# A feed-forward in 256x1024 weight tiles with tokens on partitions, and Strassen's seven products for some of the tiles

## The chip, the cores and the metric

The kernel runs on one core of one Trainium2 chip. The time is device time in microseconds (us) of one launch. The core's engines run beside each other, each through its own list of instructions in order: TensorE (PE) multiplies 128x128 blocks (a load of the stationary block, PEld, and a matmul that moves up to 512 columns past it) and adds the result up in PSUM, eight banks of 512 float32 columns; VectorE (DVE) and ScalarE (ACT) do elementwise work; SyncE (SP) issues most transfers. An instruction that needs another engine's result waits for a semaphore, and all that stands behind it on its engine waits too.

## The reference

An encoder of two layers over 256 tokens of width 2048, in float32. Each layer is an attention (a 2-D neighbourhood attention in layer 0, a dilated one in layer 1) and a feed-forward of width 8192, each with a norm ahead of it and a residual, and a last norm stands at the end:

```
def sq_relu_mlp(h, w1, w2):
    return jnp.square(jax.nn.relu(h @ w1)) @ w2
...
        x = x + sq_relu_mlp(rms_norm(x, g), w1, w2)
    return rms_norm(x, final_norm)
```

"Matrix one" below is w1 (2048 x 8192), "matrix two" w2 (8192 x 2048).

## The kernel before

**Steps.** All large products are a list of 400 steps. A step loads one block of 512 x 512 weights (1 MB, stored as four slices of 128 x 512) and multiplies with it in four quarters: 48 steps for q, k, v and 16 for the output of layer 0's attention, 72 and 8 for layer 1's, and 128 for each feed-forward. The loop at line 736 writes the program out in this order; each engine takes its instructions in that order, and nothing reorders them. Beside a step's quarters stand its tasks (a part on TensorE, then a part on the other engines), `evac` (reading of finished sums) and `post`.

**Float32 from rounded parts.** [...] A product is hi x hi + hi x lo + lo x hi. `split` (lines 103 to 105) does the cut: ACT rounds, DVE subtracts. For the weights `prep(i, u)` cuts half a block, 1024 columns at a time; in step i the two halves of step i + 2 are cut, the first after the second quarter, the second at the end. The parts lie in four buffers each (`wh`, `wl`), two steps' worth, so a cast for step i + 2 waits until TensorE has read step i's half. Then `load(i + 5)` issues the transfer of a later block, into one of three buffers.

**Matrix one** (`gemm_cols`, lines 114 to 150): the weights stand still and the tokens move. For each 128 x 128 block of weights there is a matmul of 512 columns (hi weights against both parts of the 256 tokens, line 134) and one of 256 (lo weights against hi tokens, line 136): 16 such pairs a step. Four steps sum up 512 of the 8192 hidden columns, which come out with the hidden index on partitions, as matrix two needs them. ACT copies one half of the sum (line 144), DVE adds the other (146), scales by 1/rms and takes the relu (471), ACT squares (474) and both cut the result.

**Matrix two** (`gemm_rows`, lines 160 to 175, `products`, 152): the activations stand still and 512 columns of weights move: three matmuls (lines 155 to 157) for each of two halves of the tokens and four slices, 24 a step. `add_rows` adds the sums to x (line 271).

**Order.** `ffn` (line 464) works in four groups: 16 steps of matrix one make 2048 hidden columns, 16 of matrix two use them up. At the end of a sublayer `pending_norm` transposes x for the next norm (line 194) beside the following steps; `Norm.rows` (229) multiplies to lay 1/rms along the tokens. The last two steps of all go through the first half of the tokens and then the second (`rows_apart`), and `Final.finish` (from 667) finishes a half with the last norm and writes it out.

Of the kernel before, what the change touches and what calls it, by code (L numbers as in the profile page):

```python
# [14 lines left out]
P = 128  # L15
# [13 lines left out]
class Step:  # L29
    """One weight block [4 x 128, 512], the products that it takes part in (in four  # L30
    quarters) and the work that goes with them: tasks have a part on the tensor engine
    after a quarter, evac reads the finished sums, post follows."""

    def __init__(self, src, quarters):
        self.src = src
        self.quarters = quarters
        self.evac = []
        self.tasks = [[] for _ in range(4)]
        self.post = []


@with_exitstack
def tile_encoder(ctx: ExitStack, tc: tile.TileContext, ins, out):
    nc = tc.nc

    const = ctx.enter_context(tc.tile_pool(name="const", bufs=1))
    wpool = ctx.enter_context(tc.tile_pool(name="wpool", bufs=3))
    hlpool = ctx.enter_context(tc.tile_pool(name="hlpool", bufs=4))
    big = ctx.enter_context(tc.tile_pool(name="big", bufs=9))
    mid = ctx.enter_context(tc.tile_pool(name="mid", bufs=9))  # L50
    tmp = ctx.enter_context(tc.tile_pool(name="tmp", bufs=2))
    small = ctx.enter_context(tc.tile_pool(name="small", bufs=4))
    ps_acc = ctx.enter_context(tc.tile_pool(name="ps_acc", bufs=3, space=bass.MemoryType.PSUM))
    ps_misc = ctx.enter_context(tc.tile_pool(name="ps_misc", bufs=2, space=bass.MemoryType.PSUM))
# [11 lines left out]
    rope_c = const.tile([32, T], F32, name="rope_c")  # L66
    rope_s = const.tile([32, T], F32, name="rope_s")
# [4 lines left out]
    steps = []  # L72

    def load(i):
        if i >= len(steps):
            return
        s = steps[i]
        s.w = wpool.tile([P, 4, 512], F32, name="w", tag="w")
        s.hi, s.lo = [None] * 2, [None] * 2
        if i:  # L80
            nc.sync.dma_start(s.w, s.src)

    def load_half(i, u):
        nc.sync.dma_start(steps[i].w[:, 2 * u:2 * u + 2, :], steps[i].src[:, 2 * u:2 * u + 2, :])

    def prep(i, u):
        if i >= len(steps):
            return
        s = steps[i]
        hi = hlpool.tile([P, 2, 512], F32R, name="wh", tag="wh")  # L90
        lo = hlpool.tile([P, 2, 512], F32R, name="wl", tag="wl")
        part = s.w[:, 2 * u:2 * u + 2, :]
        if i:
            split(hi, lo, part)
        else:
            for a in range(2):
                split(hi[:, a], lo[:, a], part[:, a])
        s.hi[u], s.lo[u] = hi, lo
# [15 lines left out]
    def gemm_cols(w, col, xT, nk, done):  # L114
        acc = {}
        made = []
        for k in range(nk):
            def quarter(s, n, k=k):
                if k == 0:
                    if s is steps[0]:  # L120
                        n = (0, 2, 1, 3)[n]
                    if n % 2 == 0:
                        acc[n // 2] = ps_acc.tile([P, 2, 512], F32, name="acc", tag="acc")
# [3 lines left out]
                for j in js:  # L127
                    o = acc[j // 2][:, j % 2, :]
                    cs = slice(j * P, (j + 1) * P)
                    for a in parts:  # L130
# [3 lines left out]
                        nc.tensor.matmul(o, s.hi[a // 2][:, a % 2, cs], xt.rearrange("p h t -> p (h t)"),  # L134
                                         start=first, stop=False)
                        nc.tensor.matmul(o[:, :T], s.lo[a // 2][:, a % 2, cs], xt[:, 0, :],  # L136
                                         start=False, stop=last)
            s = Step(block(w, k, col), quarter)
            steps.append(s)
            made.append(s)  # L140
        for j in range(2):
            def ev(j=j):
                b = tmp.tile([P, 2, T], F32, name="b", tag="b", bufs=2)
                nc.scalar.copy(b, acc[j][:, :, T:])  # L144
                z = tmp.tile([P, 2, T], F32, name="z", tag="z", bufs=2)
# [6 lines left out]
    def products(o, s, xt, a, ts_, start, stop):  # L152
        xh, xl = xt[:, a, 0, ts_], xt[:, a, 1, ts_]
        wh, wl = s.hi[a // 2][:, a % 2, :], s.lo[a // 2][:, a % 2, :]
        nc.tensor.matmul(o, xh, wh, start=start, stop=False)  # L155
        nc.tensor.matmul(o, xh, wl, start=False, stop=False)  # L156
        nc.tensor.matmul(o, xl, wh, start=False, stop=stop)  # L157

# [1 line left out]
    def gemm_rows(w, col, xT, ks, acc, first_k, last_k, apart=False):  # L160
        made = []
        for k in ks:
            def quarter(s, a, k=k):
                if k == first_k and a == 0:
                    tiles = [ps_acc.tile([P, 2, 512], F32, name="acc", tag="acc") for _ in range(1 + apart)]
                    for tb in range(2):
                        acc[tb] = tiles[tb * apart][:, tb, :]
# [3 lines left out]
            s = Step(block(w, k, col), quarter)  # L171
# [5 lines left out]
    class Norm:  # L177
        def __init__(self, n, perm):
            self.n, self.perm = n, perm
            self.xT = [None] * NB  # L180
            self.ss = small.tile([P, 2, NB], F32, name="ss", tag="ss", bufs=2)

        def squares(self, c):
            for tb in range(2):
                junk = tmp.tile([P, 512], F32, name="junk", tag="p", bufs=5)
# [3 lines left out]
        def transposes(self, c, half):  # L189
            self.tp = ps_misc.tile([P, 2, T], F32, name="misc", tag="misc")  # L190
# [5 lines left out]
        def parts(self, c, half):  # L196
            if half == 0:
                self.xT[c] = big.tile([P, 4, 2, T], F32R, name="xT", tag="big")
            xT = self.xT[c]
            for which, a in [(which, 2 * half + a) for which in ("hi", "lo") for a in range(2)]:  # L200
# [9 lines left out]
                elif self.perm:  # L210
                    gx = tmp.tile([P, T], F32, name="gx", tag="p", bufs=5)
# [8 lines left out]
        def rstd(self):  # L220
            r = rsqrt_mean(self.ss)
            self.r = r
            self.rw = tmp.tile([P, 2, P], F32, name="rw", tag="p", bufs=5)
            nc.vector.tensor_copy(self.rw, r.unsqueeze(2).to_broadcast([P, 2, P]))

        def rows(self):
            self.bc_ps = ps_misc.tile([P, 2, T], F32, name="misc", tag="misc")
# [4 lines left out]
        def rows_out(self):  # L232
            self.bc = small.tile([P, T], F32, name="rbc", tag="rbc", bufs=2)
# [6 lines left out]
        def cols(self):  # L240
            self.r_ps = ps_misc.tile([P, 2, T], F32, name="misc", tag="misc")
# [23 lines left out]
    # x += rows; at the end of a sublayer the next norm is begun  # L265
    def add_rows(made, col_block, acc, norm, chunk_done):
        cs = slice(col_block * 512, (col_block + 1) * 512)
        if norm is not None and norm() in fin and col_block == NB - 1:
            return
# [20 lines left out]
    def pending_norm(get):  # L290
        """Hooks behind the steps that finish x's column blocks."""
        def chunk_done(step, c):
            i = steps.index(step)
            for half in range(2):
                at(i + 1, lambda half=half: get().transposes(c, half), lambda half=half: get().parts(c, half),
                   quarter=1 + half)
            if c == NB - 1:
                at(i, None, lambda: get().rstd())
                at(i + 2, lambda: get().rows(), lambda: get().rows_out())
# [11 lines left out]
    def split_v(acc, r):  # L311
        hi = mid.tile([P, 2, 512], F32R, name="v", tag="mid")
        lo = mid.tile([P, 2, 512], F32R, name="v", tag="mid")
# [7 lines left out]
    class NaHeads:  # L321
        """Four heads: their q, k, v, bias and the steps from scores to outputs."""
# [4 lines left out]
        # bias[c + 64 e, h, o, 63 - c'] is for the query (2 t + e, c) and the key (o - 2 + 2 t, c')  # L327
        def load_bias(self, h):
            if h == 0:
                self.bias = big.tile([P, 4, 6, GRID_W], F32, name="bias", tag="big")  # L330
# [10 lines left out]
        def qk(self, which):  # L341
            t = [mid.tile([P, 4, T], F32R, name="qk", tag="mid") for _ in range(2)]
# [15 lines left out]
        def s1_pe(self, h):  # L358
            s = ps_misc.tile([P, 2, T], F32, name="misc", tag="misc")
# [5 lines left out]
        def s1_post(self, h):  # L365
            p = tmp.tile([P, 2, T], F32, name="p", tag="p", bufs=5)
# [7 lines left out]
        def s2_pe(self, h):  # L374
            pt = ps_misc.tile([P, 2, T], F32, name="misc", tag="misc")
# [6 lines left out]
        def s2_post(self, h):  # L382
            t = [tmp.tile([P, 2, T], F32R, name="pT", tag="p", bufs=5) for _ in range(2)]
# [3 lines left out]
        def s3_pe(self, h):  # L387
            o = ps_misc.tile([P, 2, T], F32, name="misc", tag="misc")
# [6 lines left out]
        def s3_post(self, h):  # L395
            if na_oT[self.c] is None:
                na_oT[self.c] = big.tile([P, 4, 2, T], F32R, name="oT", tag="big")
# [3 lines left out]
    def softmax(p):  # L401
        """p [P, 2, n]: each row of n becomes its softmax."""
# [32 lines left out]
    def rows_apart(pair, xT, acc, finish):  # L435
        """The last two blocks of a sum of four: the first half of the tokens through both, then the second."""
        for tb, s in enumerate(pair):
            def quarter(s, n, tb=tb):
                for a in (n % 2 * 2, n % 2 * 2 + 1):
                    products(acc[tb], pair[n // 2], xT[2 + n // 2], a, slice(tb * P, (tb + 1) * P),  # L440
                             False, n == 3 and a == 3)
            s.quarters = quarter
            s.evac.append(lambda tb=tb: finish(tb, acc))

    def out_rows(w, xT, nk, norm, chunk_done, order=None):
        accs = [{} for _ in range(NB)]
        last = norm is not None and norm() in fin
        order = order or [(c, k) for c in range(NB) for k in range(nk)]
# [382 lines left out]
```

## Time and profile before

| | us |
|---|---|
| median of 3 runs (2321.46 to 2324.35) | 2321.56 |
| span of the profiled execution | 2320.3 |
| TensorE waiting for the rests of weights, whole run | 3.4 |
| first feed-forward, from 408 to 1120 us | 712 |
| second feed-forward, from 1603 to 2311 us | 708 |

The runs time the execution as a whole, the span goes from the first to the last instruction. Busy times of TensorE are not additive: matmuls overlap, and one of 512 columns is busy for some 0.39 us while the next starts 0.23 us after it. A line of a view gives the line of the code, the engine, the operation, and the tiles that it writes and reads; after the bar stand busy time, mean duration and the idle time before it with what ended it.

### The profile page before, as it was taken

Reading aid. Unit: us, or ns where it says so; the run is one execution under the profiler, and the core shown is the slowest. Engines: PE = TensorE matmul, PEld = TensorE weight load, DVE = VectorE, ACT = ScalarE, POOL = GpSimd, SP = SyncE. Lnnn points to the kernel's source line nnn. Section 1 sums busy time; section 2 is a strip of 40 time slices with the busy share of each in tenths; the row PEclk is TensorE's granted clock in tenths of the full one; section 3 lists DMA queues with packets and bytes.
Section 4 is the critical chain, followed back from the end, with each engine's and each line's share of the span. In section 5 each row is a group of like instructions: output and inputs, shape, how many; then the busy total and the mean of one; then the engine's idle time right before and its main releaser. Section 6 shows DMA issues by size and latency. Waiting matters only on the chain.

```text
span 2320.3 us, 29178 instructions
## 1 busy us (share of the span) xinstructions
PE 2300.7 (99%) x11956; PEld 1963.1 (85%) x11956; DVE 1406.0 (61%) x1635; ACT 1092.6 (47%) x1390; POOL 0.7 (0%) x6
## 2 busy tenths in 40 slices
PE   8999999999999999999999999999999999999998
PEld 7888888888888888888888888888888888888886
DVE  6666765654555555566777667756654654555654
ACT  6444545543443453455444544445543543543443
POOL 0000000000000000000000000000000000000000
PEclk9999999999999999999999999999999999999999
DMA  7555655555555555555555545454555555555553
GB/s 248 169 175 176 191 182 170 182 197 200 182 187 194 185 196 189 193 181 188 189 179 184 177 164 181 164 181 169 191 192 193 182 200 187 189 187 200 200 192 135
DMA packets 73862, 430.36 MB, mean 185 GB/s; under 512 B 19776, under 2 KB 20352, under 8 KB 22528
## 3 DMA queue, kind: packets, MB, share of 16 engines
q1 hardware_dynamic: 73056, 426.80, 54.3%
q8 instruction: 93, 1.52, 0.3%
q10 hardware_dynamic: 672, 1.70, 0.2%
q14 instruction: 41, 0.34, 0.0%
HBM read 426.38 MB, written 2.10 MB: 185 GB/s over the span
## 4 chain that ended last, share of the span: by engine, by line
PE 98%; DMA 1%; DVE 1%; ACT 0%; issue 0%; SPq 0%; ACTq 0%; DVEq 0%
PE acc L134 33%; PE acc L136 17%; PE acc L156 15%; PE acc L155 15%; PE acc L157 15%; PE misc L194 1%; DMA bias<-in_rpb_dram 0%; PE misc L111 0%; PE misc L110 0%; PE misc L109 0%; DVE wl L105 0%; PE misc L593 0%; PE misc L553 0%; PE misc L380 0%; ACT wh L104 0%
## 5 line engine op out<-in xcount | busy, mean ns | idle before, releaser
L105 DVE TENSOR_TENSOR wl<-w,wh 128x1024 fp32r<-128x1024 f32 (+1 forms) x802 | 972.8, 1221 | 735.8 <-ACT wh L104 733.6
L104 ACT CAST wh<-w 128x1024 fp32r<-128x1024 f32 (+1 forms) x802 | 834.9, 1049 | 936.9 <-PE acc L157 460.2
L134 PE MATMUL acc<-xT,wh 128*128 128x512 f32 x3328 | 1178.5, 399 | 0.9 <-ACT wh L104 0.9
L136 PE MATMUL acc<-xT,wl 128*128 128x256 f32 x3328 | 935.0, 281 | 2.3 <-DVE wl L105 2.3
L134 PEld LDWEIGHTS acc<-xT,wh 128*128 128x128 f32 x3328 | 626.4, 188 | 150.4 <-ACT wh L104 1.9
L136 PEld LDWEIGHTS acc<-xT,wl 128*128 128x128 f32 x3328 | 629.8, 189 | 3.7 <-DVE wl L105 3.2
L155 PE MATMUL acc<-wh,hT 128*128 128x512 f32 x1024 | 399.5, 390 | 0.0
L156 PE MATMUL acc<-wl,hT 128*128 128x512 f32 x1024 | 399.0, 390 | 0.0
L157 PE MATMUL acc<-wh,hT 128*128 128x512 f32 x1024 | 398.9, 390 | 0.0
L157 PEld LDWEIGHTS acc<-wh,hT 128*128 128x128 f32 x1024 | 192.3, 188 | 39.9
L155 PEld LDWEIGHTS acc<-wh,hT 128*128 128x128 f32 x1024 | 192.3, 188 | 39.7
L156 PEld LDWEIGHTS acc<-wl,hT 128*128 128x128 f32 x1024 | 192.3, 188 | 39.4
L155 PE MATMUL acc<-wh,xT 128*128 128x512 f32 x320 | 126.7, 396 | 0.0
L156 PE MATMUL acc<-wl,xT 128*128 128x512 f32 x320 | 125.2, 391 | 1.1 <-DVE wl L105 1.1
L157 PE MATMUL acc<-wh,xT 128*128 128x512 f32 x320 | 124.9, 390 | 0.0
L144 ACT COPY b<-acc 128x512 f32<-128x512 f32 x104 | 60.7, 586 | 64.8 <-PE acc L136 59.1
L146 DVE TENSOR_TENSOR z<-acc,b 128x512 f32<-128x512 f32 x104 | 71.5, 691 | 25.8 <-ACT b L144 25.2
L155 PE MATMUL acc<-wh,oT 128*128 128x512 f32 x192 | 76.6, 399 | 0.0
L157 PE MATMUL acc<-wh,oT 128*128 128x512 f32 x192 | 75.0, 391 | 0.0
L156 PE MATMUL acc<-wl,oT 128*128 128x512 f32 x192 | 74.9, 390 | 0.0
L156 PEld LDWEIGHTS acc<-wl,xT 128*128 128x128 f32 x320 | 60.2, 188 | 13.1 <-DVE wl L105 1.8
L157 PEld LDWEIGHTS acc<-wh,xT 128*128 128x128 f32 x320 | 60.1, 188 | 12.5
(123 smaller groups left out, 1044.9 us busy)
## 6 DMA issues: line engine op xcount, KB each, us to landing
w<-in_ffn_w_dram SPq DMA_DIRECT2D x256, 1024.0 KB, 4.8
w<-in_dil_wqkv_dram SPq DMA_DIRECT2D x72, 1024.0 KB, 4.8
w<-in_na_wqkv_dram SPq DMA_DIRECT2D x47, 1024.0 KB, 4.9
w<-in_na_wo_dram SPq DMA_DIRECT2D x16, 1024.0 KB, 4.9
w<-in_dil_wo_dram SPq DMA_DIRECT2D x8, 1024.0 KB, 4.8
bias<-in_rpb_dram SPq DMA_DIRECT2D x32, 96.0 KB, 8.7
out_dram<-x SPq DMA_DIRECT2D x8, 256.0 KB, 2.5
x<-in_x_dram SPq DMA_DIRECT2D x3, 512.0 KB, 7.8
```

The costliest lines, as they stand in the source:

```text
L104: nc.scalar.copy(dst_hi, src)
L105: nc.vector.tensor_tensor(out=dst_lo, in0=src, in1=dst_hi.bitcast(F32), op=ALU.subtract)
L134: nc.tensor.matmul(o, s.hi[a // 2][:, a % 2, cs], xt.rearrange("p h t -> p (h t)"), start=first, stop=False)
L136: nc.tensor.matmul(o[:, :T], s.lo[a // 2][:, a % 2, cs], xt[:, 0, :], start=False, stop=last)
L144: nc.scalar.copy(b, acc[j][:, :, T:])
L146: nc.vector.tensor_tensor(out=z, in0=acc[j][:, :, :T], in1=b, op=ALU.add)
L155: nc.tensor.matmul(o, xh, wh, start=start, stop=False)
L156: nc.tensor.matmul(o, xh, wl, start=False, stop=False)
L157: nc.tensor.matmul(o, xl, wh, start=False, stop=stop)
L194: nc.tensor.transpose(self.tp[:, a, tb * P:(tb + 1) * P], x[:, tb, kt * P:(kt + 1) * P], ident)
```

## The change

Only the feed-forwards compute differently; around them buffers are laid out anew.

- **Tiles.** A step's 1 MB is now a piece of 256 x 1024 (a pair of 128-row slices k, by two blocks of 512 columns), in two transfers of 512 KB. Eight such steps sum over 2048 rows for 1024 columns and all 256 tokens (`gemm_pair`). Both matrices are multiplied with the tokens on the partitions of the result: activations stand still, weights move.
- **Plain steps** (kind "s") have the 24 matmuls of matrix two before. Their weights are cut as before.
- **Strassen steps** (kind "x") treat the tile as a 2 x 2 block matrix against 2 x 2 blocks of activations (two halves of the tokens, two slices k) and form seven block products for eight: 21 matmuls of 512 columns in quarters of 6, 6, 6 and 3. They use Winograd's sums: four of weights (`prep_x`) and three of activations (`sums_and_parts`). In matrix one the tiles 3 and 5 of each eight are Strassen steps, in matrix two 3, 5 and 6. In matrix two's second block of a group the order of the tiles is 0, 3, 1, 5, 2, 6, 4, 7; layer 0's last group keeps the plain order there, and layer 1's last has 0, 3, 1, 5, 6, 2, 4, 7.
- **`prep`** is spread over a step: for an x tile of step i + 2 the sums after quarter 0 of step i, its own second half and the rounding of the sums after quarter 1, their rest after quarter 2, the slice left over at the end.
- **PSUM.** All eight banks are in use: four for the block sums that plain products add to, four for products that Strassen's scheme combines. After the last x step `begin` combines them into a tile C, in the last step `end` adds the others quarter by quarter. Before, sums came in three pairs of banks and two single ones served the transposes; in the feed-forward these now borrow banks.
- **Hidden values** come out with tokens on partitions: ACT scales by 1/rms, takes the relu and squares, in the first step of the next block; in its second and third step TensorE transposes them in four groups of four, and they are cut, for tiles 3, 5 and 6 with the sums. The multiplication that laid 1/rms along the tokens remains for layer 1's attention and layer 0's first norm alone.
- **Buffers** of attention and feed-forward are now two pools that take each other's place (`Part`).

```
     def prep_x(s, n):
         w = s.w
         if n == 0:
             t = s.sums = part.pool.tile([P, 4, 512], F32, name="sums", tag="sums", bufs=1)
             add(nc.vector, t[:, 0:2, :], w[:, 1:3, :], w[:, 0, :].unsqueeze(1).to_broadcast([P, 2, 512]))
             add(nc.vector, t[:, 2, :], t[:, 1, :], w[:, 1, :])
             add(nc.vector, t[:, 3, :], t[:, 2, :], w[:, 3, :])
         elif n == 1:
             hi, lo = two_parts(s, 1)
             split(hi, lo, w[:, 2:4, :])
             s.hs = part.pool.tile([P, 4, 512], F32R, name="hs", tag="hs", bufs=2)
             nc.scalar.copy(s.hs, s.sums)
         elif n == 2:
             ls = part.pool.tile([P, 4, 512], F32R, name="ls", tag="ls", bufs=2)
             subtract(nc.vector, ls, s.sums, s.hs.bitcast(F32))
...
         else:
             hi, lo = two_parts(s, 0)
             split(hi[:, 1, :], lo[:, 1, :], w[:, 1, :])
...
     X = (("1", "A11", 2), ("2", "A12", 3), ("6", "S2", 6), ("7", "S3", 4), ("5", "S1", 5), ("4", "A22", 7),
          ("3", "S4", 1))
...
             if kind == "x":
                 def quarter(s, m, pair=pair, n=n):
                     for bank, a, b in X[2 * m:2 * m + 2]:
                         product(bank, left(pair, a), (s.hi[b], s.lo[b]), n == first_x[-1] and bank in "1567")
...
     def begin(m):
         if m == 0:
             C = q["C"] = part.pool.tile([P, 4, 512], F32, name="C", tag="C")
             nc.scalar.copy(C[:, 0, :], q["1"])
             q["U"] = scratch([P, 512], "U")
             subtract(nc.vector, q["U"], q["6"], C[:, 0, :])
         elif m == 1:
             subtract(nc.vector, q["C"][:, 2, :], q["U"], q["7"])
...
     s = made[first_x[-1] + 1]
     for m in range(4):
         s.after[0 if s is made[-1] else m].append(lambda m=m: begin(m))
         if not split_end:
             made[-1].after[m].append(lambda m=m: end(m))
...
 def sums_and_parts(raw, t, half, sums):
     c = scratch([P, 3, P], "c")
     a11, a21, a12, a22 = raw[:, 0, :P], raw[:, 0, P:], raw[:, 1, :P], raw[:, 1, P:]
     subtract(nc.vector, c[:, 0, :], a11, a21)
     subtract(nc.vector, a21, a21, a22)
     subtract(nc.vector, c[:, 1, :], a11, a21)
     subtract(nc.vector, c[:, 2, :], a12, c[:, 1, :])
     hi, lo = (t[:, 2 * half:2 * half + 2, h, :] for h in range(2))
     nc.scalar.copy(hi, raw)
     nc.scalar.copy(sums[:, 0], c)
     subtract(nc.vector, lo, raw, hi.bitcast(F32))
     subtract(nc.vector, sums[:, 1], c, sums[:, 0].bitcast(F32))
...
 FF_PAIRS, FF_PAIRS2 = (3, 5), (3, 5, 6)
...
         for n in range(4):
             s.quarters(s, n)
             for pe, post in s.tasks[n]:
                 pe()
+            for f in s.after[n]:
+                f()
...
+            elif i and n < 3:
+                prep(i + 2, n)
             for pe, post in s.tasks[n]:
                 post()
```

More of the change, by code (lines that the diff above doesn't have):

```diff
@@ L482, in tile_encoder, with both @@
+            def both(q, tb):
+                return q["C"][:, 2 * tb:2 * tb + 2, :].rearrange("p a n -> p (a n)")
+            for cp in range(2):
+                end = last and next_norm() in fin and cp == 1
+                order = (0, 3, 1, 5, 6, 2, 4, 7) if end else (0, 3, 1, 5, 2, 6, 4, 7) if cp and not last else range(8)
+                gemm_pair(w2g, cp, hT, sums, ff_order(FF_PAIRS2, order),
+                          lambda made, q, cp=cp: residual(made, q, cp), split_end=end)
     ffn(norms[1], ins["ffn0_w1"], ins["ffn0_w2"], lambda: norms[2], begin_norm(2, True))
+    parts[len(steps)] = "attention"
@@ L736, in tile_encoder @@
     for i, s in enumerate(steps):
+        now["i"] = i
+        if i in parts:
+            part.begin(parts[i])
         if i == 1:
```

420 lines of the change are left out of this document (294 added, 126 removed).

## The prediction

> **What bounds the kernel now.** I read the page first: span, busy times, chain.
>
> ```profile
> span 2320.3 us, 29178 instructions
> ...
> PE 2300.7 (99%) x11956; PEld 1963.1 (85%) x11956; DVE 1406.0 (61%) x1635; ACT 1092.6 (47%) x1390; POOL 0.7 (0%) x6
> ...
> PE 98%; DMA 1%; DVE 1%; ACT 0%; issue 0%; SPq 0%; ACTq 0%; DVEq 0%
> ```
>
> TensorE carries 98% of the chain. The execution took 1.3 us less inside its span than the median of 2321.56, so I subtract from the median. Then the windows (columns: length; busy and count of PE, PEld, DVE, ACT, POOL; clock; DMA): the first feed-forward, and the worst stretch of the attention.
>
> ```profile
> 408.00:1120.00 712.00, 712.00 (x3619) 604.97 (x3618) 405.70 (x421) 331.46 (x387) 0.00 (x0) 1.00 0.55 189
> 73.00:81.00 8.00, 6.49 (x28) 4.58 (x27) 6.65 (x10) 2.98 (x6) 0.00 (x0) 1.00 0.03 13
> ```
>
> In the feed-forward TensorE never stops, VectorE (DVE) has 57% and ScalarE (ACT) 47%. So the time there is a number of matrix products times their spacing, as long as DVE delivers the weights' second parts. Spacings come from the DVE timeline, where sums leave at the end of every fourth step (start, length, line, tiles):
>
> ```profile
> 430.77 1.39 DVE L146 TENSOR_TENSOR z<-acc,b 128x512 f32<-128x512 f32 x2 [0.51 <-ACT b L144]
> 452.95 1.39 DVE L146 TENSOR_TENSOR z<-acc,b 128x512 f32<-128x512 f32 x2 [0.50 <-ACT b L144]
> ...
> 519.19 1.28 DVE L271 TENSOR_TENSOR x<-x,acc 128x512 f32<-128x512 f32 x2 [0.41 <-PE acc L157]
> ...
> 584.47 1.28 DVE L271 TENSOR_TENSOR x<-x,acc 128x512 f32<-128x512 f32 x2 [0.41 <-PE acc L157]
> 606.98 1.40 DVE L146 TENSOR_TENSOR z<-acc,b 128x512 f32<-128x512 f32 x2 [0.55 <-ACT b L144]
> ...
> 674.82 1.41 DVE L146 TENSOR_TENSOR z<-acc,b 128x512 f32<-128x512 f32 x2 [0.55 <-ACT b L144]
> ```
>
> Matrix one takes 22.18 us per four steps in the first group and (674.82 - 606.98)/3 = 22.61 in later ones. Matrix two takes (584.47 - 519.19)/3 = 21.76 for 96 products of 512 columns: 0.2267 us each, 5.44 a step.
>
> **The change: TensorE.** A layer now takes 4 x 22.18 + 12 x 22.61 + 16 x 21.76 = 708.2 us. Afterwards every product has matrix two's form. A plain step has 24, a Strassen step 21 (4.76 us). Matrix one has 16 Strassen steps of 64 a layer: 1488 products; matrix two 24 of 64: 1464. 2952 x 0.2267 = 669.1. The hidden values now have tokens on partitions and must be transposed: 32 groups of four a layer. The chain shows one such group, and the broadcast of 1/rms that norms 1 and 3 no longer need:
>
> ```profile
> 1054.39 0.44 PE misc L194 x4
> ...
> 416.49 0.45 PE misc L229 x4
> ```
>
> 32 x 0.44 = 14.1, so 683.2 a layer: 25.0 saved, 50.0 in two layers, and 2 x 0.45 for the broadcasts: **51 us**. If nothing else changed, 2270.5.
>
> **The change: DVE and ACT.** A plain tile costs each engine two passes of 1024 columns. A Strassen tile needs sums of weights (1024, 512, 512 columns on DVE), their rounding (2048, ACT) and rest (2048, DVE), and 1024 + 512 of its own. Durations by form (us busy, mean ns), then the timeline for what back-to-back instructions take:
>
> ```profile
> L105 DVE TENSOR_TENSOR wl<-w,wh 128x1024 fp32r<-128x1024 f32 x798 | 970.2, 1223 | 735.8 <-ACT wh L104 733.6
> L105 DVE TENSOR_TENSOR hT<-z,hT 128x512 fp32r<-128x512 f32 x64 | 41.4, 689 | 38.7 <-ACT hT L104 38.7
> L368 DVE TENSOR_TENSOR p<-misc,bias 128x256 f32<-128x256 f32 x32 | 12.0, 417 | 0.0
> L338 DVE TENSOR_TENSOR bias<-bias,namask 128x1536 f32<-128x1536 f32 x4 | 7.0, 1758 | 23.4 <-DMA bias<-in_rpb_dram 15.8 <-DMA w<-in_na_wqkv_dram 7.6
> ```
>
> ```profile
> 436.04 1.29 DVE L105 TENSOR_TENSOR hT<-z,hT 128x512 fp32r<-128x512 f32 x2 [1.21 <-ACT hT L104]
> 437.52 2.36 DVE L105 TENSOR_TENSOR wl<-w,wh 128x1024 fp32r<-128x1024 f32 x2 [0.18 <-ACT wh L104]
> ...
> 1140.43 0.29 DVE L496 TENSOR_SCALAR ra<-rbc 128x256 f32<-128x256 f32 x1
> 1140.75 0.42 DVE L497 TENSOR_TENSOR rb<-ra,rope_s 32x256 f32<-32x256 f32 x1
> ```
>
> ```profile
> L104 ACT CAST wh<-w 128x1024 fp32r<-128x1024 f32 x798 | 832.6, 1051 | 936.9 <-PE acc L157 460.2 <-PE acc L134 452.4 <-issue 9.2
> ...
> L474 ACT ACTIVATE z<-z 128x512 f32<-128x512 f32 x64 | 39.5, 633 | 60.6 <-DVE z L471 60.6
> ...
> L104 ACT CAST wh<-w 128x512 fp32r<-128x512 f32 x4 | 2.3, 623 | 0.0
> ...
> L690 ACT ACTIVATE x<-x,fr 128x512 f32<-128x512 f32 x4 | 2.7, 716 | 1.4 <-DVE fr L680 1.4
> ```
>
> Independent instructions overlap: 1024 columns cost 2.36 - 1.22 = 1.14, 512 cost 1.29 - 0.69 = 0.60. One that reads its forerunner's result costs its full length plus 0.03. No row has 2048 columns: 1536 less 1024 is 0.535, so 1.758 + 0.535 = 2.29, 2.21 overlapped. 128 columns: 0.417 - (0.689 - 0.417)/2 = 0.28. ACT's 2048: 1.05 + 2 x 0.43 = 1.91.
>
> [...]
>
> A plain tile: 2.28. A Strassen tile: sums 2.6, own rest 1.14, the 2048 rest 2.21, last 0.60 = 6.55; and the big rest waits for ACT, which starts on the sums at 2.7 and ends at 4.6 while DVE is free at 3.74: 0.89 of waiting, 7.44. Behind that wait on DVE stand the tile's last part and the next tile; TensorE waits for both. TensorE gains 0.68 for it.
>
> The stretch that decides is matrix two. Block A (steps 0 to 7, Strassen at 3, 5, 6) and B (8 to 15, at 9, 11, 13). Preparation runs two steps ahead. Step 0: ACT does eight relu and square passes (pairs of about 1.28), then the last cast of tile 2, so DVE leaves step 0 at 9.3 us, 3.9 after TensorE (5.44). DVE from there: step 1, tile 3, one transposed part (0.60, inside the wait) and one with sums (four of 128, one of 512, one of 384: 2.2) 9.67; step 2, 2.23 + 0.60 + 2.28 = 5.11; steps 3 and 4, tiles 5 and 6, 14.88; step 5, 2.28; step 6, 2.28 + 0.5 waiting for TensorE; step 7, where Strassen's recombination (2.52), the bank sums (2.40), the residual (2.28) and tile 9 (6.55) meet, 13.75; step 8, 2.28; step 9, tile 11 to the end of the big rest, 6.93. Sum 57.7, of which 3.5 are waits.
>
> TensorE would reach tile 11's second quarter after six plain steps, four Strassen steps, four transposes and 1.6: 32.6 + 19.0 + 1.8 + 1.6 = 55.0. So it is delayed 3.9 + 57.7 - 55.0 = **6.6 us a group**; with no wait counted 3.1. Smaller delays within (step 6, the last transposed bank at step 3) lie inside this. Matrix one: 33.5 a block on DVE (4 more with transposed parts) against 186 x 0.2267 = 42.2; no delay.
>
> I take the middle, 4.85: rows with full waits (1.21) are of a DVE that is ahead, the row of one behind (437.52) has 0.18; neither is nearer. 8 x 4.85 = 38.8. The last group of each layer has the next norm's work beside block B (6.9 and 2.4 us of DVE): I add 5 together. Tail:
>
> ```profile
> 2305.91 0.69 DVE L669 TENSOR_TENSOR x<-x,acc 128x512 f32<-128x512 f32 x1 [3.13 <-PE acc L157]
> ...
> 2308.92 0.74 DVE L687 SCALAR_TENSOR_TENSOR x<-x,fr,gf 128x512 f32<-128x512 f32 x1
> 2311.34 0.69 DVE L669 TENSOR_TENSOR x<-x,acc 128x512 f32<-128x512 f32 x1 [1.68 <-PE acc L157]
> ```
>
> The first half's finish holds DVE 3.75 us and began 5.43 before the second; it will begin 2.72 before: 1.0 more. 2321.6 - 51 + 38.8 + 5 + 1 = **2315**.
>
> At nothing I cost: loads (two of 512 KB for one of 1 MB), queued on SP behind the freed tile:
>
> ```profile
> w<-in_ffn_w_dram SPq DMA_DIRECT2D x256, 1024.0 KB, 4.8
> ```
>
> They land in 4.8, and DVE comes to the tile two steps of its own, about 10 us, later; uncovered, each late load costs the difference. ACT's added passes: below 60%, behind DVE in the stretch. The pools that change hands: attention's order is the same; between 0 and 5 us.
>
> **Rivals.** *DVE keeps up.* The gain stays whole: 2321.6 - 51 + 1 = 2272, with delays at the layers' ends some 2276. For it: matrix two averages 40.9 of DVE a block (3 x 7.44 + 5 x 2.28 + 7.2) against 41.5. Against it: block A's 5.7 of transposed parts and the lag of 3.9.
>
> *DVE bounds matrix two, every wait in full* (slower): 8 x 6.6 + 7 = 60, so 2331, to 2342 with DVE 3% slower. It decides from 6.2 us a group, where the 51 are used up. For it: waits for ACT are the commonest wait of DVE now (733.6 us). Against it: only three of the waits have nothing to fill them.
>
> *The clock falls in the gaps.*
>
> ```profile
> 2290.00:2321.00 31.00, 21.31 (x95) 17.31 (x93) 13.49 (x25) 10.61 (x19) 0.00 (x0) 0.90 0.20 76
> ```
>
> With 9.7 us idle the clock is 0.90; in the window from 73 to 81, with 1.5 idle, 1.00. Half speed for as long as the 6.6 idle would add some 50: 2380. [...]
>
> That the products don't get fewer can't be: the order of steps fixes them.
>
> **How the numbers follow.** A measurement of this kernel can tell about 0.2% (4.6 us) from no change. Forecast (2302 to 2327) 0.45; DVE keeps up 0.22; DVE bounds in full 0.30; clock 0.03. The forecast lies about 0.25 below 2317, 0.18 within 0.2%, 0.02 above. Faster 0.22 + 0.25 = 0.47, same 0.18, slower 0.02 + 0.30 + 0.03 = 0.35. The range 2278 to 2340 leaves out half the first rival, the far end of the second and the clock, 0.2.
>
> **What would show it.** Matmuls: 11956 less 504 a layer and 8 = 10940. Steps of 5.44 and 4.76 where TensorE doesn't wait. TensorE waiting 30 to 60 us in all for the big rests and rests of tiles 5, 6, 9, 11 of matrix two, none in matrix one; DVE near 78% busy. Wrong, if those waits are under 10 us (first rival), if matrix one waits too, or if products of the new form are not 0.2267 apart.

## The result, and the profile after

The changed kernel takes 2358.98 us (median, 2357.72 to 2363.37) against 2322.22 for the kernel before in the same runs: ratio 1.016, 95% interval 1.0145 to 1.0174. The prediction was 2315 with a range to 2340: it had the wrong side, and the time lies above the range.

The page of the changed kernel (busy time, share of the span, count by engine; then the chain by engine; then two groups of instructions with busy time, mean ns and idle before):

```profile
span 2357.5 us, 28402 instructions
...
PE 2283.7 (97%) x10940; PEld 1893.7 (80%) x10940; DVE 1835.7 (78%) x2186; ACT 1243.3 (53%) x1558; POOL 0.7 (0%) x6
...
PE 74%; DVE 14%; ACT 7%; issue 3%; DMA 2%; SPq 0%; ACTq 0%; DVEq 0%
...
L176 ACT CAST hs<-sums 128x2048 fp32r<-128x2048 f32 x80 | 153.0, 1913 | 264.3 <-DVE sums L136 264.3
...
L133 DVE TENSOR_TENSOR ls<-sums,hs 128x2048 fp32r<-128x2048 f32 x80 | 183.3, 2292 | 51.1 <-ACT hs L176 51.1
```

1016 matmuls are gone, as foreseen, and TensorE's share of the chain fell from 98 to 74%: VectorE (DVE) and ScalarE (ACT) took its place. The two durations that no row of before had, 2.29 and 1.91 us, came out as estimated. The waits of TensorE (what waited, for what: total, times, longest):

```profile
PE banks L195 <- DVE hT L191: 23.2, 8, 2.9
PE banks L196 <- DVE ls L133: 14.3, 19, 1.5
PE banks L196 <- DVE wl L191: 6.2, 17, 0.8
PE banks L384 <- DMA x<-in_x_dram: 5.6, 2, 4.7
PE banks L384 <- DVE x L136: 5.5, 2, 2.8
```

The largest had been called a smaller one: once a group, the product that needs a bank lent to the fourth group of transposes waits until DVE has cut it into `hT`. Rests (`ls`, `wl`: what the rounding leaves over) are the second, and the two waits for `x` stand at the end of layer 0. How long is a group? ACT's copies that open each recombination (line 336; start, length) stand at fixed steps: two of matrix one, two of matrix two.

```profile
620.34 0.58 ACT L336 COPY C<-banks 128x512 f32<-128x512 f32 x1
...
664.77 0.58 ACT L336 COPY C<-banks 128x512 f32<-128x512 f32 x1
...
718.57 0.58 ACT L336 COPY C<-banks 128x512 f32<-128x512 f32 x1
...
757.71 0.58 ACT L336 COPY C<-banks 128x512 f32<-128x512 f32 x1
...
800.09 0.58 ACT L336 COPY C<-banks 128x512 f32<-128x512 f32 x1
```

A group takes 800.09 - 620.34 = 179.75 us. Its 738 products at 0.2267 and eight groups of transposes at 0.44 are 170.8, so **8.95 us a group** are lost. From 664.77 to 718.57, which holds the first steps of block A, there are 53.8 us for some 48.7 of TensorE's work; from 718.57 to 757.71 39.1 for 36.0; the rest, matrix one, is within 0.7 of its products.

DVE's timeline in block A of that group (start, length, ..., idle before and its releaser) shows what it is doing:

```profile
697.79 0.68 DVE L191 TENSOR_TENSOR hT<-banks,hT 128x512 fp32r<-128x512 f32 x1
...
704.17 2.29 DVE L133 TENSOR_TENSOR ls<-sums,hs 128x2048 fp32r<-128x2048 f32 x1 [0.84 <-ACT hs L176]
...
711.63 2.29 DVE L133 TENSOR_TENSOR ls<-sums,hs 128x2048 fp32r<-128x2048 f32 x1 [0.84 <-ACT hs L176]
```

At every big rest of tiles 5 and 6 of block A DVE stands still for 0.84 us, as the walk had it with 0.89. Where other work of DVE stands between the sums and their rest the wait is short or nothing, at tile 3 of block A and at the first Strassen tile of block B:

```profile
688.62 2.29 DVE L133 TENSOR_TENSOR ls<-sums,hs 128x2048 fp32r<-128x2048 f32 x1 [0.24 <-ACT hs L176]
...
727.95 2.29 DVE L133 TENSOR_TENSOR ls<-sums,hs 128x2048 fp32r<-128x2048 f32 x1
```

The same stretch of block A on TensorE, and the windows around it and around the same place one group earlier (length; busy and count of PE, PEld, DVE, ACT, POOL; clock; DMA share; GB/s):

```profile
695.24 0.39 PE L197 MATMUL banks<-hs 128*128 128x512 f32 x1
698.53 0.80 PE L195 MATMUL banks<-hs,hT 128*128 128x512 f32 x1 [2.90 <-DVE hT L191]
699.12 0.63 PE L196 MATMUL banks<-ls,hT 128*128 128x512 f32 x1
699.55 0.63 PE L197 MATMUL banks<-hs,hT 128*128 128x512 f32 x1
...
702.01 0.39 PE L197 MATMUL banks<-wh,hs 128*128 128x512 f32 x1
702.24 0.39 PE L195 MATMUL banks<-wh,hT 128*128 128x512 f32 x1
```

```profile
510.00:520.00 10.00, 7.10 (x34) 5.53 (x33) 9.34 (x18) 6.54 (x10) 0.00 (x0) 1.00 0.35 105
...
690.00:700.00 10.00, 7.10 (x31) 5.50 (x30) 9.34 (x18) 6.55 (x10) 0.00 (x0) 0.92 0.35 105
700.00:710.00 10.00, 10.00 (x42) 8.16 (x40) 9.02 (x10) 3.80 (x4) 0.00 (x0) 0.91 0.56 145
```

After the wait of 2.90 us products stand 0.43 apart instead of 0.23, until 702: half the clock, for some 3.4 us (granted clock 0.52 from 698.5 to 702, 1.00 from 702 to 705). One group earlier, after as long a wait (2.90 us, to 518.84), the clock stayed at 1.00. Over the run it fell behind five of the eight such waits; what decides it these views do not show.

### The profile page after: what moved, and what is told of

Same layout as the page of the kernel before. It is cut to its first block, busy times and chain, and to the rows that moved or that the text cites. A ratio compares the mean times of both kernels' runs of the same rounds, so it can differ in the third digit from the quotient of the medians.

```text
span 2357.5 us, 28402 instructions
## 1 busy us (share of the span) xinstructions
PE 2283.7 (97%) x10940; PEld 1893.7 (80%) x10940; DVE 1835.7 (78%) x2186; ACT 1243.3 (53%) x1558; POOL 0.7 (0%) x6
## 4 chain that ended last, share of the span: by engine, by line
PE 74%; DVE 14%; ACT 7%; issue 3%; DMA 2%; SPq 0%; ACTq 0%; DVEq 0%
PE banks L196 18%; PE banks L197 18%; PE banks L195 18%; PE banks L220 12%; PE banks L222 6%; DVE sums L136 4%; DVE wl L191 3%; DVE ls L133 3%; ACT wh L190 2%; ACT hs L176 2%; DMA bias<-in_rpb_dram 1%; DVE C L136 1%; ACT C L682 1%; PE banks L384 1%; PE banks L695 1%
## 5 line engine op out<-in xcount | busy, mean ns | idle before, releaser
L191 DVE TENSOR_TENSOR wl<-w,wh 128x1024 fp32r<-128x1024 f32 (+1 forms) x802 | 920.7, 1165 | 349.6 <-ACT wh L190 346.9
L220 PE MATMUL banks<-xT,wh 128*128 128x512 f32 x1280 | 454.7, 399 | 0.5 <-ACT wh L190 0.4
L195 PE MATMUL banks<-wh,xT 128*128 128x512 f32 x1152 | 453.6, 394 | 0.0
L196 PE MATMUL banks<-wl,xT 128*128 128x512 f32 x1152 | 448.7, 389 | 1.0 <-DVE wl L191 1.0
L197 PE MATMUL banks<-wh,xT 128*128 128x512 f32 x1152 | 449.4, 390 | 0.0
L222 PE MATMUL banks<-xT,wl 128*128 128x256 f32 x1280 | 358.1, 280 | 2.3 <-DVE wl L191 2.3
L195 PE MATMUL banks<-wh,hT 128*128 128x512 f32 x736 | 292.1, 397 | 2.2 <-ACT wh L190 2.2
L196 PE MATMUL banks<-wl,hT 128*128 128x512 f32 x736 | 288.9, 393 | 2.4 <-DVE wl L191 2.4
L197 PE MATMUL banks<-wh,hT 128*128 128x512 f32 x736 | 288.6, 392 | 0.0
L220 PEld LDWEIGHTS banks<-xT,wh 128*128 128x128 f32 x1280 | 241.1, 188 | 55.4 <-ACT wh L190 1.4
L197 PEld LDWEIGHTS banks<-wh,xT 128*128 128x128 f32 x1152 | 216.2, 188 | 45.8
L195 PEld LDWEIGHTS banks<-wh,xT 128*128 128x128 f32 x1152 | 216.5, 188 | 42.8
L222 PEld LDWEIGHTS banks<-xT,wl 128*128 128x128 f32 x1280 | 241.9, 189 | 4.0 <-DVE wl L191 3.7
L133 DVE TENSOR_TENSOR ls<-sums,hs 128x2048 fp32r<-128x2048 f32 x80 | 183.3, 2292 | 51.1 <-ACT hs L176 51.1
L195 PEld LDWEIGHTS banks<-wh,hT 128*128 128x128 f32 x736 | 139.4, 189 | 30.8 <-ACT wh L190 2.6
L197 PEld LDWEIGHTS banks<-wh,hT 128*128 128x128 f32 x736 | 139.0, 189 | 29.6
```

Source lines behind the costliest of these rows:

```text
L133: engine.tensor_tensor(out=out, in0=a, in1=b, op=ALU.subtract)
L191: nc.vector.tensor_tensor(out=dst_lo, in0=src, in1=dst_hi.bitcast(F32), op=ALU.subtract)
L220: nc.tensor.matmul(o, s.hi[a][:, cs], xt.rearrange("p h t -> p (h t)"), start=first, stop=False)
L222: nc.tensor.matmul(o[:, :T], s.lo[a][:, cs], xt[:, 0, :], start=False, stop=last)
```

## The experiments

Theories, as the expectations name them. **A**: in matrix two DVE works through its list in order, with waits for ACT in it, and is the bound; TensorE's wait for the bank lies inside DVE's lag. **B**: the wait for the bank, and the half clock after it, come on top. **C**: the loss doesn't hang on matrix two's number of tiles, but sits in the new layout or in the form of a Strassen tile; each expectation says what it would give.

### The bank read early

In block A the third and fourth groups of transposes both come after the first quarter of the third step, and the fourth is cut first, so that its bank is free early. The core of the edit:

```diff
-                    at(i + 1 + r // 2, pe, post, quarter=r % 2 * 2)
+                    hooks.append((pe, post))
+                (pe0, post0), (pe1, post1), (pe2, post2), (pe3, post3) = hooks
+                at(i + 1, pe0, post0, quarter=0)
+                at(i + 1, pe1, post1, quarter=2)
+                at(i + 2, lambda: (pe2(), pe3()), lambda: (post3(), post2()), quarter=0)
```

> In the third step of matrix two's first block (and of matrix one's second) the third and fourth groups of transposes are both made after the first quarter, and the fourth is cut before the third, so that the bank it borrows is read before the Strassen step needs it; nothing is added or left out. Theory A (the sum of VectorE's work with its in-order waits sets matrix two; the 2.9 us wait for the bank and the 3.4 us of half clock behind it lie inside that lag): TensorE waits later instead, for rests of tiles 5 and 6, and the time falls by 0 to 9 us from 2359, to 2350 to 2359. Theory B (the bank wait and the clock drop add to the path: 2.9 + 1.7 us in each of 8 groups = 37): 2322. In both the 2.9 us waits and the clock below 1.00 at this place go.

Measured: 2362.48 us, ratio to before 1.0173 (1.0144 to 1.0203), 3 us above A's band and within the spread of the changed kernel's runs (to 2363.37). TensorE's waits:

```profile
PE banks L196 <- DVE ls L133: 29.4, 32, 1.5
PE banks L196 <- DVE wl L191: 15.3, 33, 0.6
...
PE banks L195 <- DVE hT L191: 2.2, 8, 0.3
```

The wait for the bank went from 23.2 to 2.2 us, and those for rests rose by 24.2 together. The clock fell in three stretches of the run instead of seven (by windows of 10 us, the tail left out), and the time did not fall. So B falls: whatever TensorE loses at that place it would have lost a step or two later, because DVE is late. The half clock was hidden in the same lag.

### Two tiles in matrix two

```diff
-    FF_PAIRS, FF_PAIRS2 = (3, 5), (3, 5, 6)
+    FF_PAIRS, FF_PAIRS2 = (3, 5), (3, 5)
```

> Matrix two has Strassen steps at tiles 3 and 5 alone (2 of 8 for 3 of 8). TensorE's sum rises by 8 groups x 2 blocks x 3 products x 0.2267 = 10.9 us, VectorE's falls by 5.2 us a block and 1.6 us of sums of activations. Theory A: no lag is left in matrix two beyond a bank wait under 1 us a group; 2322 - 51 + 10.9 + 1.5 (tail) + 5 (end of layer 0) + some 10 = 2300, 2290 to 2308. Theory B: the bank is still read late and the clock still falls: 37 on top of 2289, 2326. Theory C (the new form of the products or the layout loses the time, not Strassen's sums): 2359 + 11 = 2370.

Measured: 2312.02 us, ratio 0.9955 (0.9935 to 0.9974), faster than before and 4 us above A's band. The third tile, whose products alone would save 10.9 us, makes the kernel 47.0 slower. TensorE's waits for `ls` are 2.1 us in the whole run, but not every wait is gone:

```profile
PE banks L195 <- DVE hT L191: 7.0, 8, 0.9
...
PE banks L196 <- DVE ls L133: 2.1, 2, 1.4
```

Part of the 4 us shows in the spacing of products in a Strassen step. Its first product and its sixteenth on TensorE's timeline:

```profile
599.07 0.39 PE L195 MATMUL banks<-hs,xs 128*128 128x512 f32 x1
...
602.55 0.39 PE L195 MATMUL banks<-wh,xT 128*128 128x512 f32 x1
```

15 products in 3.48 us are 0.232 apart, not the 0.2267 of plain steps. Over 80 Strassen steps of the changed kernel that is 80 x 15 x 0.0053 = 6.4 us. Why they stand further apart is open.

### The rests left out

This kernel leaves out the rest of the weight sums: Strassen's products read the rounded sums in its place. DVE's 2.29 us a tile and the wait before them go, and the products stay as many.

```diff
-            ls = part.pool.tile([P, 4, 512], F32R, name="ls", tag="ls", bufs=2)
-            subtract(nc.vector, ls, s.sums, s.hs.bitcast(F32))
             for a in range(4):
-                s.hi[4 + a], s.lo[4 + a] = s.hs[:, a, :], ls[:, a, :]
+                s.hi[4 + a], s.lo[4 + a] = s.hs[:, a, :], s.hs[:, a, :]
```

> Leaves out the rest of the weight sums of Strassen tiles (the 2048-column subtraction on VectorE; the rounded sums are read in its place, so TensorE does the same products): 2.2 us and the 0.84 us wait ahead of it less on VectorE per Strassen tile, nothing else. Theory A: VectorE's chain in matrix two falls by about 4 x 3 = 12 us a group against a lag of 9, so TensorE hardly waits: 2322 - 51 + 1.5 + 5 + some 8 = 2285, 2276 to 2296. Theory B: the bank is read later than the step needs it as before, 37 stay: 2315. Theory C: 2350 or more.

One run gave 2306.6 us: 52 less than the change, 10 above A's band. The rest and the wait ahead of it are what cost the time; what A had left out are the spacing above (6 us) and waits that stayed:

```profile
PE banks L193 <- DVE hT L189: 9.5, 8, 1.2
...
PE banks L382 <- DVE x L136: 5.5, 2, 2.8
```

### The layout alone

Both lists of Strassen tiles are empty (`FF_PAIRS, FF_PAIRS2 = (), ()`), and the finished sums are copied out of the banks in place of the recombination.

> The new tiles and layout with no Strassen step at all (the sums are copied from the banks to C by VectorE): 3072 products a layer for 2952, the transposes stay. By products: a layer 3072 x 0.2267 + 14.1 = 710.5 against 708.2 before, in two layers 4.6 more, 0.9 less for the broadcasts, 1.5 tail, 5 at the end of layer 0: 2332, 2324 to 2340, with no waits for rests in the feed-forward. Theories A and B both say this; theory C (the layout or the form of the products is what costs) says 2355 or more.

Measured: 2330.23 us, ratio 1.0034 (1.002 to 1.0047). The products' count and plain spacing, the transposes and the new buffers are priced rightly to 2 us; C falls as far as it put the loss in the layout.

### Strassen in matrix one alone

`FF_PAIRS, FF_PAIRS2 = (3, 5), ()`, matrix two as in the last kernel.

> Strassen's products for tiles 3 and 5 of matrix one as in the change, none in matrix two. Theory A (VectorE's work in matrix two, with its in-order waits, is what costs; matrix one has room): the layout alone gave 2330.2; 32 Strassen steps save 32 x 0.68 = 21.8, and their products stand 0.231 apart rather than 0.2267, which gives back 32 x 0.1 = 3: 2311.5 (2308 to 2315), no rest of a weight waited for in the feed-forward. Theory C (a Strassen tile costs about as much as it saves wherever it stands): 2322 to 2332.

Measured: 2310.98 us, ratio 0.9953 (0.9938 to 0.9967), on A's figure. In matrix one a tile pays in full. When the residual is added to x (DVE line 136; start, length), the group that lies between is 890.08 - 714.56 = 175.5 us:

```profile
714.56 2.35 DVE L136 TENSOR_TENSOR x<-x,C 128x1024 f32<-128x1024 f32 x2
...
890.08 2.35 DVE L136 TENSOR_TENSOR x<-x,C 128x1024 f32<-128x1024 f32 x2
```

### The third tile moved to matrix one

`FF_PAIRS, FF_PAIRS2 = (3, 5, 6), (3, 5)`: as many products as the change.

> The third Strassen tile is moved from matrix two to matrix one: 3 of 8 in matrix one, 2 of 8 in matrix two; products as many as in the changed kernel. Theory A: matrix one's DVE has 33.5 + 5.2 = 38.7 us a block against 41.5 of TensorE, but the second block also cuts the transposed parts of the first (4 us), 42.7, so it falls behind by 1 to 4 us a group; against 2312.0 with two tiles in each: 2312 - 10.9 + 0.8 + 8 x (1 to 4) = 2310 to 2334, middle 2318. If only the mean work over a group counted (two blocks of each matrix, under TensorE's time): 2302. If the third tile costs the same anywhere: 2359.

Measured: 2330.21 us, ratio 1.0034 (1.0021 to 1.0047), inside A's band at its upper end. The third tile costs 18 net there, 47 in matrix two. The sum of DVE's work over a group (the second possibility) does not decide; it decides block by block. TensorE waits in this kernel's matrix one too:

```profile
661.85 0.50 PE L196 MATMUL banks<-wl,xT 128*128 128x512 f32 x1 [0.57 <-DVE wl L191]
664.97 0.50 PE L196 MATMUL banks<-ls,xs 128*128 128x512 f32 x1 [1.45 <-DVE ls L133]
```

### Two tiles, and the bank read early

The first experiment's edit on the kernel with two tiles in each matrix.

> Two Strassen tiles of 8 in both matrices, and the third and fourth groups of transposes of a block both after the first quarter of the third step, the fourth's bank read first. With two tiles VectorE isn't behind, and the waits for that bank (7.0 us in all in the profile with two tiles) stand alone: theory A takes them away without another wait in their place: 2312.0 less 5 to 8, so 2304 to 2308. Theory B' (as in the changed kernel, another wait of the same block takes their place): 2310 to 2314.

Measured: 2311.55 us, ratio 0.9952 (0.9936 to 0.9969): no gain, as B' said; A's 2304 to 2308 is missed. TensorE waits for `hT` sixteen times instead of eight, up to 0.3 us, 4.5 in all, and 0.9 us more for `ls`. The two groups of transposes now stand together, and each of their cuts is waited for a little.

### The sums on GpSimd

The three instructions of the weight sums move from `nc.vector` to `nc.gpsimd`.

> The changed kernel with the three instructions of the weight sums on GpSimd. Theory A: 2.6 us a Strassen tile leave VectorE, 7.8 of the 8.95 us that a group loses; leaving the rests out (2.2 us a tile and 0.84 of waiting) gave 2306.6, so 2300 to 2315 here, if GpSimd makes a tile's sums in the 10 us of two steps. Rival: GpSimd takes over 10 us a tile, or VectorE's instructions lengthen while it works: the rounding on ScalarE waits for the sums, the rest behind it, and the time is over 2359.

Measured: 2416.56 us, ratio 1.0407 (1.0386 to 1.0428): the rival, though for its second reason. GpSimd's rows, one of DVE that reads SBUF twice and one that reads a bank and SBUF, in this kernel (busy us, mean ns):

```profile
L136 POOL TENSOR_TENSOR sums<-sums,w 128x512 f32<-128x512 f32 x160 | 292.2, 1826 | 12.5
L136 POOL TENSOR_TENSOR sums<-w 128x1024 f32<-128x1024 f32 x80 | 202.8, 2535 | 1872.8 <-DMA w<-in_ffn_w_dram 1184.5 <-DVE wl L191 495.2 <-DVE ls L133 152.9
...
L191 DVE TENSOR_TENSOR wl<-w,wh 128x1024 fp32r<-128x1024 f32 x718 | 966.7, 1365 | 363.4 <-ACT wh L190 361.0
L133 DVE TENSOR_TENSOR U<-banks,C 128x512 f32<-128x512 f32 x32 | 21.9, 683 | 0.0
```

and DVE's in the changed kernel:

```profile
L191 DVE TENSOR_TENSOR wl<-w,wh 128x1024 fp32r<-128x1024 f32 x718 | 867.8, 1221 | 349.6 <-ACT wh L190 346.9
L133 DVE TENSOR_TENSOR U<-banks,C 128x512 f32<-128x512 f32 x32 | 21.9, 683 | 0.0
```

A tile's sums take GpSimd 2.54 + 2 x 1.83 = 6.2 us, under the 10 that were allowed. But DVE's `wl` went from 1221 to 1365 ns on average while `U`, with one input in PSUM, stayed at 683; over 718 instructions that is 99 us of DVE. The sums also come 3.6 us later than from DVE, and everything behind them waits (DVE idles for 98.2 us before `ls`, 51.1 in the changed kernel). Other subtractions with both inputs in SBUF grew as well, `c<-h` of 128x128 from 288 to 627 ns on average, while `ls` stayed (2292 and 2290); why, no run shows. At one place on the two timelines a `c<-h` takes 2.54 us and ends 0.15 us after GpSimd's sum:

```profile
697.89 2.54 DVE L133 TENSOR_TENSOR c<-h 128x128 f32<-128x128 f32 x1
...
697.88 2.40 POOL L136 TENSOR_TENSOR sums<-w 128x1024 f32<-128x1024 f32 x1 [4.82 <-DVE h L133]
```

### The rounding and the rest in halves

ACT's rounding of the sums and DVE's rest become two passes of 1024 columns each, so that DVE's first half no longer waits for ACT.

```diff
-            nc.scalar.copy(s.hs, s.sums)
+            for a in (0, 2):
+                nc.scalar.copy(s.hs[:, a:a + 2, :], s.sums[:, a:a + 2, :])
...
-            subtract(nc.vector, ls, s.sums, s.hs.bitcast(F32))
+            for a in (0, 2):
+                subtract(nc.vector, ls[:, a:a + 2, :], s.sums[:, a:a + 2, :], s.hs[:, a:a + 2, :].bitcast(F32))
```

> The changed kernel, with the rounding of the sums on ScalarE and the rest on VectorE each cut in two passes of 1024 columns instead of one of 2048. VectorE's first half of the rest can then start 1.05 us after the sums and need not wait; its work grows by about 0.07 us a tile. This asks how much of a group's 8.95 us are waits for ScalarE. Theory A as the prediction's walk has it (3.5 of the 57.7 us are waits, and each comes in full): 8.95 - 3.5 + 0.3 = 5.8 a group, 2359 - 25 = 2334 (2328 to 2342). Rival, that VectorE's work alone bounds matrix two and its waits are refilled behind: 2354 to 2361.

Measured: 2343.89 us median (2338.25 to 2344.61), ratio 1.0085 (1.007 to 1.01). DVE's row of the rests, with its idle time before them:

```profile
L133 DVE TENSOR_TENSOR ls<-sums,hs 128x1024 fp32r<-128x1024 f32 x160 | 188.3, 1219 | 0.0
```

51.1 us of idling became 0.0, at 5 us more work; DVE's idling for ACT before `wl` rose from 346.9 to 379.0, so not all of it became time. 15 us were gained by the medians, nearer A's 25 than the rival's 5 at most, but 2 above A's band. The profiled execution is the fastest, 2338.25 against 2359.31 of the changed kernel's, 21 less. TensorE's waits and one window of it:

```profile
PE banks L197 <- DVE hT L193: 21.1, 8, 2.6
...
PE banks L198 <- DVE wl L193: 4.8, 15, 0.6
PE banks L198 <- DVE ls L133: 2.7, 8, 0.6
```

```profile
870.00:880.00 10.00, 9.13 (x34) 7.39 (x35) 9.90 (x12) 5.29 (x7) 0.00 (x0) 0.83 0.47 147
```

The group with this window took 178.5 us, the two before, without a fall of the clock, 177.0 each. Here DVE's lag no longer covers the slow products, and they count. In the changed kernel the first two groups took 179.7 and 179.75, the first without such a fall and the second with one.

### One tile in matrix two; a plain last group

`FF_PAIRS, FF_PAIRS2 = (3, 5), (5,)`:

> Two Strassen tiles of 8 in matrix one, one (tile 5) in matrix two. One tile a block saves 2 x 0.68 a group, less 0.2 for the spacing of its products; the bank waits cost up to 1.0 a group and the last group up to 1.3 a layer: 2311 - 8 x (0.2 to 1.1) + 2 x (0 to 1.3) = 2302 to 2312, middle 2306. If a Strassen tile in matrix two costs what it saves whatever the number: 2311 to 2312.

Measured: 2303.16 us, ratio 0.9915 (0.9899 to 0.9932), inside the expected 2302 to 2312 near its lower end. Waits for `hT` and `ls` are no longer among TensorE's. Against none in matrix two, one tile gains 7.8 of the 9.6 us that 16 Strassen steps save after their wider spacing (10.9 less 16 x 15 x 0.0053).

Two tiles, but plain ones in matrix two of each layer's last group:

> Two Strassen tiles of 8 in both matrices, but none in matrix two of the last group of each layer. With two tiles a group took 174.77 us, with none in matrix two 175.5, and yet a layer as long (706.35 against 706.73), because the last group, where the next norm's squares and transposed parts stand beside block B, gives back 2 us (TensorE waits 1.38 and 0.76 there for the rests of tiles). Theory A: the three first groups keep their 0.75, the last gives nothing back: 2311 - 2 x 2.3 = 2306.5 (2304 to 2309). If the loss isn't in the last group: 2311 to 2313.

Measured: 2307.07 us, ratio 0.9933 (0.9918 to 0.9947), on A's figure: 5 us of what two tiles lost lay in the last groups, where the next norm's work stands beside them. In the kernel with two tiles throughout, TensorE's timeline there reads:

```profile
1085.10 0.50 PE L196 MATMUL banks<-ls,hs 128*128 128x512 f32 x1 [1.38 <-DVE ls L133]
1096.54 0.50 PE L196 MATMUL banks<-ls,hs 128*128 128x512 f32 x1 [0.76 <-DVE ls L133]
```

### All three remedies

Halves, the bank read early and the plain last group, at the change's number of tiles:

> The change's number of tiles (2 of 8, 3 of 8) with every stall found so far removed: the sums' rounding and rest in halves, the third and fourth groups of transposes together with the fourth's bank read first, and plain tiles in matrix two of each layer's last group. What is left is VectorE's work. Theory A: the first two leave 2338 to 2344 (as in the run with halves alone, since the bank's wait lies inside VectorE's lag), the plain last group gives back 6 a layer inside the feed-forward and the 2.7 to 5 of the wait for x behind it: 2321 to 2332, middle 2327, so no faster than before. If the stalls, and not VectorE's work, were the cause: 6 groups x 5.4 + 2 x 2.7 below the layout's 2330.2, with 8 for the spacing: 2300.

Measured: 2320.32 us, ratio 0.999 (0.9981 to 1.0), just under A's band and 20 above what remains if the stalls were the whole cause. What TensorE still waits for:

```profile
PE banks L198 <- DVE wl L193: 9.1, 25, 0.6
...
PE banks L198 <- DVE ls L133: 5.4, 12, 0.6
```

And with two tiles in matrix two:

> The same three remedies with 2 of 8 in both matrices (but for matrix two of the last groups). VectorE isn't behind here, so nothing should be left but the products' spacing: against 175.5 us a group with Strassen in matrix one alone, 172.2 + 1.2 = 173.4 plus up to 0.9: 2311 - 6 x (1.2 to 2.1) = 2298 to 2304, so at or below the 2303.2 of one tile. If waits are refilled here too: 2307, as without the first two remedies.

Measured: 2302.0 us, ratio 0.9911 (0.9895 to 0.9928), inside the expected 2298 to 2304, the fastest kernel of the study, and not to be told from the one with a single tile (2303.16). The median times by the number of Strassen tiles in matrix two, with two in matrix one:

| tiles of 8 in matrix two | without remedies | with all three |
|---|---|---|
| 0 | 2310.98 | |
| 1 | 2303.16 | |
| 2 | 2312.02 | 2302.0 |
| 3 (the change) | 2358.98 | 2320.32 |

With the remedies the third tile still makes the kernel 18 us slower, though its products alone would save 7 (12 steps, 0.68 each, less their spacing): with the stalls found so far taken out, what TensorE waits for there is DVE's own work. In the second group's block A and the start of B, from 680 to 730 us, DVE idles for 1.0 us in all.

## Why the prediction was wrong

- **TensorE's 51 us.** The count was right, and without Strassen the sum came out to 2 us. Strassen's products at the plain 0.2267 were mis-sized: 0.232, some 6 us over the run.
- **DVE's and ACT's prices.** Right: 2.292 and 1.913 us, and 0.84 of waiting for the 0.89 worked out; only a transposed part with its sums took 2.43 (690.82 to 693.25) for 2.2.
- **The walk through matrix two.** Right in order and place, and a little short: from 683.97, where DVE leaves step 0, to 742.83, the end of step 11's big rest, it took 58.9 us, where the walk with all its waits had 57.7. Half of the 1.1 is the transposed parts with sums, half waits for casts. The walk gave 6.6 us a group with every wait in full; TensorE's gaps and slow products in the group above add up to 7.4 us, the wider spacing adds 0.8, and 0.8 of the 8.95 I can't place.
- **"I take the middle, 4.85"** is the step that failed: it put half of the walk's 3.5 us of waits a group at nothing. DVE's row of 0.18 idle behind a late DVE was of a cut whose rounding needs nothing from DVE, so ACT can run ahead with it. The rest of the sums waits however late DVE is, since ACT can't begin to round before DVE has made them. The timeline shows these waits one by one as the walk had them: 0.84 us at steps 5, 6 and 11, 0.24 at step 3, none at step 9. These are 2.8 us a group, 22 in eight groups. Halving the passes removed all such idling (51 us with matrix one's) and 15 us of time by the medians, more than half of the 22; a group without a fall of the clock became 2.7 us shorter, nearly all of its 2.8. Of the 8 x (8.95 - 4.85) = 33 us that a group's term was short, the middle is 8 x (6.6 - 4.85) = 14; the other 19 are what the walk left out, the 1.1 us above and the wider spacing above all.
- **The layers' ends, 5 us,** were mis-sized. Both feed-forwards lose 82.2 us (727.5 and 725.9 long against 712.5 and 709.7 before, where 25.5 a layer should have gone); 8 x 8.95 are 71.6 of it, so the last groups cost 10.6 more, and layer 1's attention took 486.8 instead of 482. Of these 5, some 3 stand in the layout alone, too (484.7 there, where TensorE waits for `gx`); the other 2 go with x coming late, for which TensorE waits 2.7 us there and 0.3 in the layout alone. 15 in place of 5.
- **The bank at step 3 "lies inside this".** Right, and the first experiment shows it, though it is TensorE's longest wait in the profile. It uses up the lag first: TensorE waits 20.5 us for rests (14.3 and 6.2), short of the sign of 30 to 60, and 44.7 with the bank read early.
- **Matrix one no delay.** Right (2310.98), and close to its limit: one tile more and it waits.
- **The rivals.** "DVE bounds in full, 2331 to 2342" was what happened, short by the walk's 1.1 us a group, the last groups and the spacing. "The clock falls in the gaps" happens too, behind five of the eight waits for the bank, but not with its price: 1.5 us (178.5 against 177.0 for a group, with the passes in halves), hidden while DVE is the bound.

Together: 2270.5 + 71.6 + 10.6 + 5 and 1 for the tail are 2358.7.

## What to carry to other kernels

Where one engine makes a value, a second rounds it and the first takes the rest, the wait belongs to every such tile that has no other work of the first engine between: it doesn't vanish when the first engine is behind (0.84 us a time here), and it goes if both passes are cut in halves (51.1 us in the run, then 0.0). When work moves from the bound engine to its helper, add it up block by block, with the busiest block and the last one by themselves, and put tiles in one at a time: here one in matrix two gained 8 us, the second needed three remedies to cost nothing, and the third cost 47. The longest wait in a profile need not be worth anything: ask whether its releaser is behind anyway.

## What the runs showed of the hardware

In the changed kernel products stood 0.43 us apart instead of 0.23 for about 3.4 us, with a granted clock of 0.50 to 0.55 over it, after five of eight idle times of 2.89 to 2.90 us and not after the other three; they did so, too, after one of 2.79 us (at 1088 us) and after two of 2.19 and 0.76 us close together (at 2313 us). The first 15 products of a Strassen step stood 0.232 us apart and those of plain steps 0.2267, with no wait recorded between them. GpSimd took 2.54 us for an addition of 128 x 1024 that takes DVE 1.22. In that kernel DVE's `wl` grew from 1221 to 1365 ns on average and `c<-h` from 288 to 627; `ls`, which reads SBUF twice as they do, did not (2292, 2290), nor did `U`, with one input in PSUM (683).
